# Last layer norm of a hybrid encoder step: the products by the scale moved from VectorE to GpSimd for all row blocks but the last, whose Newton steps go to GpSimd

## The chip, the core and the metric

The kernel runs on one core of a Trainium2 chip. The metric is device time in microseconds (us); lower is better. Engines are named as in the profile: PE is TensorE (matmuls), PEld its weight loads, DVE is VectorE, ACT is ScalarE, POOL is GpSimd, SP is SyncE, whose queue issues the transfers between the core's memory (SBUF) and DRAM.

## The reference, cut to what matters

One layer of an encoder trunk for two groups of requests: 1024 prompt tokens and 8 x 16 sample tokens, 1152 rows of 1024 features in all. Three mixers (windowed attention and two linear recurrences) read one projection and are merged; a layer norm; a feed-forward part with 2816 hidden features; a second layer norm, whose result is the output. All inputs and outputs are float32.

```python
def layer_norm(x, g, b):
    xf = x.astype(F32)
    mu = xf.mean(-1, keepdims=True)
    var = jnp.square(xf - mu).mean(-1, keepdims=True)
    return ((xf - mu) * lax.rsqrt(var + LN_EPS) * g.astype(F32) + b.astype(F32)).astype(x.dtype)
...
    up, new_ffn_conv = causal_dwconv(x @ w_up, buf_ffn, f_conv_w)
    gate, val = jnp.split(up + f_conv_b, 2, axis=-1)
    x = layer_norm(ALPHA * x + (jax.nn.silu(gate) * val) @ w_down, ln2_g, ln2_b)
```

Only this last `layer_norm` is touched by the change.

## The kernel before

The 1152 tokens are nine row blocks of 128 (`NT` = 9): blocks 0 to 7 are the prompt, block 8 is the sample. In the feed-forward part the hidden features stand on partitions; the down-projection then brings the tokens back onto partitions. Its sums are kept in SBUF, in nine tiles `yac` of 128 tokens x 1024 features.

The hidden features are taken 256 at a time; the last call of `down` takes the last 512 of them. For each row block and each half of 512 columns it runs twelve matmuls into a PSUM bank (tag `g`, five banks in this phase), and VectorE adds the bank to `yac` (L1758). Behind each row block stands `beside(last_ln(j))`: the layer norm of that block is a generator that is moved on in steps between the matmuls of the blocks that follow. `yield 3` in it lets three such steps pass.

In `last_ln` of blocks 0 to 7:

- `normalise` takes the statistics of both halves on VectorE (L321), joins them (L322), adds the epsilon (L324), and computes the inverse root in `rsqrt`: an integer seed (L302, L303) and three Newton steps of three VectorE operations each (L307, L308, L310), all on 128x1; then `shifted` makes -mean/deviation (L331), and ScalarE scales and shifts the block (L336).
- Three VectorE products by the scale `g2` (L1787) and three POOL additions of `b2` (L1788) follow, on thirds of 384, 384 and 256 columns, then one store of 512 KB.

Block 8 has nothing behind it and has its own branch: the statistics and Newton steps on VectorE at raised priority, `(y - mean) g` in three VectorE operations (L1779), `times 1/deviation, plus b` in three more (L1781), and a store after each third.

The order on each engine is laid down when the kernel is built: a scheduler with its own timeline places the instructions of all engines, and each engine then takes its queue strictly in that order, waiting on semaphores. In the kernel before, the scheduler interleaves the Newton steps of one block with the additions and statistics of the next ones.

Of the kernel before, what the change touches and what calls it, by code (L numbers as in the profile page):

```python
# [10 lines left out]
F32 = mybir.dt.float32  # L11
F32R = mybir.dt.float32r
I32 = mybir.dt.int32
# [4 lines left out]
P = 128  # L18
# [27 lines left out]
def shape_constants():  # L46
    c = np.zeros((P, CW), np.float32)
    s = np.arange(P)[:, None]
    t = np.arange(P)[None, :]

    def put(n, v):
        o, w = CO[n]
        c[:, o:o + w] = v

    put("ident", s == t)
    put("ui", s <= t)
    same = (s // TB) == (t // TB)
    put("us", (s <= t) & same)
    put("bm", same)
    put("negp", np.where(s <= t, 0.0, -1e30))  # L60
    put("negs", np.where((s <= t) & same, 0.0, -1e30))
    k = np.arange(2 * P)[None, :]
    put("nega", np.where(((s < 64) & (k >= 192)) | ((s >= 64) & (k < 64)), -1e30, 0.0))
    # s in the first half of a pair of blocks of b, t in its second half; columns for the second halves alone
    for b in (1, 2, 4, 8, 16):
        r = ((s // (2 * b)) == (t // (2 * b))) & ((s // b) % 2 == 0)
        put(f"r{b}", r.reshape(P, -1, 2, b)[:, :, 1].reshape(P, 64))
    return c
# [3 lines left out]
def tile_encoder_step(ctx: ExitStack, tc: tile.TileContext, cst, x_prompt, x_sample, cache_k, cache_v, st_hgrn,  # L72
# [18 lines left out]
    # the banks of PSUM, shared out anew for each phase  # L91
# [22 lines left out]
    def load_in_turn(out, in_):  # L114
        """not ahead of the loads that come before"""
        tc.keep_in_program_order(nc.sync.dma_start(out=out, in_=in_))

# [35 lines left out]
    def halves_of(x, b):  # L153
        """[P, a, 128] -> [P, a, pairs, 2, b]"""
        return x.rearrange("p a (n h t) -> p a n h t", h=2, t=b)

    def put_seconds(x, b, ps):
        """the columns of the second halves, where s lies in the first half of the same pair"""
        m = x.shape[1]
        V.copy_predicated(halves_of(x, b)[:, :, :, 1, :],  # L160
                          reg(b).rearrange("p (o n t) -> p o n t", o=1, t=b).to_broadcast([P, m, 64 // b, b]),
                          ps.rearrange("p a (n t) -> p a n t", t=b))
# [6 lines left out]
    # per-feature vectors, features on partitions  # L169
# [29 lines left out]
    def prep(pieces, kt=KD, cols=P):  # L199
        """pieces: (part of the raw tile, DRAM view [p, k, c]); the exact two-part split of the weights"""  # L200
        raw = wp.tile([P, KD, P], F32, tag="wraw", name=nm("wraw"), bufs=2)
        for sel, ap in pieces:
            load(sel(raw), ap)
        hl = wp.tile([P, 2, KD, P], F32R, tag="whl", name=nm("whl"), bufs=2)
        S.copy(hl[:, 0, :kt, :cols], raw[:, :kt, :cols])  # L205
        V.tensor_sub(hl[:, 1, :kt, :cols], raw[:, :kt, :cols], hl[:, 0, :kt, :cols].bitcast(F32))  # L206
        return hl
# [5 lines left out]
    # work that runs beside the large products: generators, moved on between their parts  # L213
# [18 lines left out]
    def block(hl, xh, xl, n, evict, kt=KD):  # L232
        """features on partitions: [128 columns of the weights, 384 tokens]"""
# [11 lines left out]
    def row_block(lh, ll, rhs, evict):  # L245
        """tokens on partitions: [128 tokens, 512 columns of the weights]"""
# [10 lines left out]
    class Queue:  # L257
        """Blocks of the large products in order; the weights of the next unit are made ahead."""
# [40 lines left out]
    def rsqrt(pool, x, n):  # L299
        """x ** -0.5 on [P, n]: an integer seed and three Newton steps"""  # L300
# [13 lines left out]
    def ln_group(pool, tiles, eps):  # L314
        """tiles: for each, its two halves of 512 features, tokens on partitions -> means and 1 / deviation"""
# [12 lines left out]
    def shifted(pool, mu, rs):  # L328
        """-mean / deviation"""
# [8 lines left out]
    def to_features(pool, xns, n, gname, bname, hi, lo):  # L338
        """normalised rows of three tiles -> scaled, features on partitions, in two parts"""
# [12 lines left out]
    # -mean / deviation and 1 / deviation of each input row: the residual is made anew from the input  # L352
# [40 lines left out]
    def bc(x, n, w=P):  # L393
        """[P, n] -> [P, n, w]"""
        return x.rearrange("p (c o) -> p c o", o=1).to_broadcast([P, n, w])

    def rowb(x, n, w=P):
        """[P, w] -> [P, n, w]"""
# [5 lines left out]
    # ======== A: banded attention with sinks ========  # L404
# [28 lines left out]
    # the first two units: the tokens that are ready first  # L433
# [23 lines left out]
    # the norm weights carry the half of silu = x (1 + tanh(x/2)) / 2  # L457
# [27 lines left out]
    def a_parts(j):  # L485
        """queries: their two parts on the two halves of the partitions; keys: the first part on both halves, and
        the second; so a product of 128 rows and one of 64 make a score"""
# [160 lines left out]
    # ======== common to B and C ========  # L648
    # group n: tokens 384 n..; its units of 128 tokens; in the last group the third unit is the samples
# [3 lines left out]
    def ev_silu2(store_to, tag, bufs):  # L653
        """x (1 + tanh(x/2)): twice silu"""
# [7 lines left out]
    def finish_group(oT, fac, wcol, z2, out):  # L662
        """o in rows per token -> normalised, gated, features on partitions"""
# [14 lines left out]
    def sample_cross(st, pair):  # L678
        """[P, b, n, 16] against each sample's state -> features on partitions, PSUM [v, b, n, 16]"""
# [6 lines left out]
    def sample_state(st, el, kT, w, out):  # L686
        """S_b <- e_b S_b + k_b^T w_b, and out it goes"""
# [11 lines left out]
    # ======== C: gated delta rule ========  # L699
    cg = {}  # L700

    def c_gates():
# [45 lines left out]
        # softplus: max(x, 0) + log1p(exp(-|x|))  # L748
# [42 lines left out]
    def ev_conv(ci, pre_fn, done):  # L791
        """causal convolution of width 4 and twice silu; the pieces follow one another"""
# [64 lines left out]
    def c_units(hd):  # L857
        """v, q, k; the gate z comes later"""
# [13 lines left out]
    def c_pre(hd, n):  # L872
# [9 lines left out]
        # norms of q and k (twice silu both)  # L882
# [18 lines left out]
        # the rows (v - e^cum k S) / |k| go through (I + N)^-1 with N = (k k^T dec) beta / |k|^2 by columns,  # L901
        # then times beta / |k|: w of the reference
# [13 lines left out]
        # v in rows per token (twice silu), by |k|  # L916
# [5 lines left out]
        # decays between tokens, [s, t]  # L922
# [22 lines left out]
        # (I - M)^-1: blocks of 16 by substitution, a block per partition  # L945
# [38 lines left out]
    def c_levels(hd, n):  # L984
# [15 lines left out]
        # 16 -> 32  # L1000
# [18 lines left out]
        # 32 -> 64  # L1019
# [16 lines left out]
        # 64 -> 128  # L1036
# [89 lines left out]
    def c_finish(hd, n):  # L1126
        x, h = hd.g[n], hd.h
        # q was left unnormalised: n = o rq' rsqrt(rq'^2 mean(o^2) + eps), rq' = rq / sqrt(128)
# [10 lines left out]
    # ======== B: gated linear attention with a decay per key feature ========  # L1139
    def b_consts():  # L1140
# [6 lines left out]
        # lower bounds: softmax over the layers, running sum less the first layer's  # L1147
# [13 lines left out]
    def b_units(hd):  # L1161
# [3 lines left out]
        # f = lb + (1 - lb) sigmoid(x) = (1 + lb e) / (1 + e) with e = exp(-x), at least 1e-30  # L1165
# [34 lines left out]
    def b_pre(hd, n):  # L1200
# [10 lines left out]
        # q and k against the ends of the chunk  # L1211
# [20 lines left out]
        # s = t, and neighbours  # L1232
# [25 lines left out]
    def b_levels(hd, n):  # L1258
        """every pair (s, t) of a chunk at the level whose halves part it"""
# [88 lines left out]
    def b_finish(hd, n):  # L1348
        x, h = hd.g[n], hd.h
        # o is doubled  # L1350
# [5 lines left out]
    # ======== the order of the mixers ========  # L1356
# [114 lines left out]
    def branch_units(br, follow):  # L1471
        """the parts of the next branch's o take the place of this one's"""
# [36 lines left out]
    def pair(m, dst):  # L1509
        """w_branch rows of the last branch, columns of blocks m and m + 1"""  # L1510
# [40 lines left out]
    def rows_h(j):  # L1551
        """the residual, doubled as the mix is"""
# [11 lines left out]
    def mix_split(stage):  # L1564
        """mix = mh + ml; a step uses two pieces and frees one, each n of the branch before has freed eight"""
# [206 lines left out]
    def last_ln(j):  # L1772
        y = yac[j]
        if j == NT - 1:
            # nothing follows: each third goes out as it is ready, ((y - mean) g) / deviation + b
            with tc.high_priority(400):
                (mu, rs), = ln_group(fp, [[y[:, :512], y[:, 512:]]], LN_EPS)
                for sl, gg in zip(thirds, g2):
                    V.scalar_tensor_tensor(y[:, sl], y[:, sl], mu, gg, ALU.subtract, ALU.mult)  # L1779
                for sl, bb in zip(thirds, b2):  # L1780
                    V.scalar_tensor_tensor(y[:, sl], y[:, sl], rs, bb, ALU.mult, ALU.add)  # L1781
                    store(y_s.rearrange("b t d -> (b t) d")[:, sl], y[:, sl])
            return
        normalise(fp, y, LN_EPS)
        yield 3
        for sl, gg, bb in zip(thirds, g2, b2):
            V.tensor_mul(y[:, sl], y[:, sl], gg)  # L1787
            G.tensor_add(y[:, sl], y[:, sl], bb)  # L1788
        store(y_p[0, j * P:(j + 1) * P, :], y)

    pairs = [ffn_pair(i) for i in range(NFF)]
    # the first two units: the tokens that are ready first
# [47 lines left out]
```

## Time and profile before

| | |
|---|---|
| time, median of 3 runs | 2320.24 us (2312.8 to 2323.56) |
| span of the profiled execution | 2315.3 us |
| busy share of PE / DVE / ACT / POOL over the span | 97% / 65% / 40% / 4% |
| granted TensorE clock, mean | 0.988 |
| last normalise step of block 7 on ACT starts | 2304.97 us |

For the profiled execution only the span, from its first to its last instruction, is recorded; no time of its own stands beside it. Times in the traces are us from the start of the span. A row of single instructions has start, duration, engine, line, operation, `written<-read` and the tile's shape; in brackets stands how long the engine had been idle before it and what ended that. On VectorE successive rows overlap a little, so the distance from start to start says what an instruction costs the queue.

### The profile page before, as it was taken

The page shows a single profiled execution, that of the slowest core. Times are in us where ns is not written, and L with a number is a line of the kernel's source. Part 1 is how long each engine was busy: PE and PEld are TensorE (multiplying, and loading weights), DVE is VectorE, ACT ScalarE, POOL GpSimd, SP SyncE. Part 2 cuts the span into 40 slices and gives each one's busy share as a digit, 9 for nine tenths or more (in the row PEclk, how much of TensorE's full clock was granted, in tenths as well). Part 3 has the DMA queues.
Part 4 walks back from the last instruction along what each step waited for, and adds up shares of the span by engine and source line. Part 5 has one row for each costly group of instructions (what it writes and reads, how often), then busy time and mean ns, then how long its engine had stood idle before and what let it go on. Part 6 is the DMA issues. An engine that isn't in the chain of part 4 may idle for free.

```text
span 2315.3 us, 35344 instructions
## 1 busy us (share of the span) xinstructions
PE 2256.6 (97%) x13297; PEld 2101.9 (91%) x13297; DVE 1504.4 (65%) x4324; ACT 927.5 (40%) x2106; POOL 102.8 (4%) x74
## 2 busy tenths in 40 slices
PE   6999999999999999999999999999999999999996
PEld 6988989999999999999999978999999999999994
DVE  7256446667675657766777797676566566656669
ACT  4356434434344446354532333453334333432331
POOL 2000000000000000000000054000000000000004
PEclk9999989999999999999999999999999999999998
DMA  4111222222222221222354552321111110111112
GB/s 132 46 55 43 80 74 62 65 80 67 63 82 60 70 63 54 68 66 78 98 151 134 174 165 74 139 65 47 38 29 56 47 47 21 56 52 42 38 47 82
DMA packets 223836, 168.46 MB, mean 73 GB/s; under 512 B 34427, under 2 KB 213409, under 8 KB 223649
## 3 DMA queue, kind: packets, MB, share of 16 engines
q1 hardware_dynamic: 223664, 166.21, 24.0%
q8 instruction: 104, 1.70, 0.3%
q14 instruction: 68, 0.55, 0.1%
HBM read 126.91 MB, written 40.11 MB: 72 GB/s over the span
## 4 chain that ended last, share of the span: by engine, by line
PE 87%; DVE 7%; ACT 3%; DMA 2%; issue 1%; SPq 0%; POOL 0%; DVEq 0%; ACTq 0%
PE psg L107 72%; PE psp L107 6%; PE psch L107 4%; PE psp L147 2%; PE psms L107 2%; PE psch L147 1%; PE psms L147 1%; DVE yac L1787 1%; DVE lnst L321 1%; DMA x<-d_g 1%; ACT L1185 1%; ACT L1181 0%; DVE nwa L308 0%; DVE nwy L310 0%; DVE whl L206 0%
## 5 line engine op out<-in xcount | busy, mean ns | idle before, releaser
L107 PE MATMUL psg<-hh,whl 128*128 128x384 f32 x2976 | 812.6, 346 | 0.0
L107 PE MATMUL psg<-x1h,whl 128*128 128x384 f32 x2112 | 545.0, 336 | 1.2 <-ACT whl L205 1.2
L107 PEld LDWEIGHTS psg<-hh,whl 128*128 128x128 f32 x2976 | 537.7, 189 | 8.7 <-issue 3.6
L107 PE MATMUL psg<-hl,whl 128*128 128x384 f32 x1488 | 511.3, 344 | 1.5 <-POOL hl L347 1.3
L107 PEld LDWEIGHTS psg<-x1h,whl 128*128 128x128 f32 x2112 | 382.8, 188 | 3.2 <-ACT whl L205 1.5
L107 PE MATMUL psg<-x1l,whl 128*128 128x384 f32 x1056 | 355.5, 337 | 0.6 <-POOL x1l L347 0.6
L107 PEld LDWEIGHTS psg<-hl,whl 128*128 128x128 f32 x1488 | 281.5, 189 | 5.1 <-POOL hl L347 1.6
L107 PE MATMUL psg<-late,g 128*128 128x512 f32 x1080 | 251.2, 391 | 0.0
L107 PEld LDWEIGHTS psg<-late,g 128*128 128x128 f32 x1080 | 201.9, 188 | 42.9
L107 PEld LDWEIGHTS psg<-x1l,whl 128*128 128x128 f32 x1056 | 198.9, 188 | 1.7 <-POOL x1l L347 0.9
L206 DVE TENSOR_TENSOR whl<-wraw,whl 128x1024 fp32r<-128x1024 f32 (+1 forms) x122 | 144.2, 1183 | 68.0 <-ACT whl L205 66.9
L1758 DVE TENSOR_TENSOR yac<-yac,psg 128x512 f32<-128x512 f32 x180 | 123.5, 687 | 91.4 <-PE psg L107 88.0
L107 PE MATMUL psg<-o,whl 128*128 128x384 f32 x720 | 140.1, 345 | 3.1 <-DVE x L1464 1.7
L205 ACT CAST whl<-wraw 128x1024 fp32r<-128x1024 f32 (+1 forms) x122 | 121.4, 995 | 48.0 <-PE psg L107 24.7
L107 PEld LDWEIGHTS psg<-o,whl 128*128 128x128 f32 x720 | 125.8, 191 | 6.7 <-issue 2.1
L107 PE MATMUL psg<-wres,mixh 128*128 128x512 f32 x288 | 92.8, 395 | 3.6 <-DVE x L1464 2.7
L1718 DVE SCALAR_TENSOR_TENSOR va<-xp,fvec,va 128x384 f32<-128x384 f32 x132 | 82.0, 622 | 19.8 <-ACT va L1715 18.1
L1718 DVE SCALAR_TENSOR_TENSOR ga<-xp,fvec,ga 128x384 f32<-128x384 f32 x132 | 81.6, 620 | 8.2 <-ACT ga L1715 6.6
L1747 ACT CAST late<-wraw 128x1024 fp32r<-128x1024 f32 x20 | 20.1, 1047 | 162.6 <-PE psg L107 162.6
L1699 ACT COPY xp<-psg 128x384 f32<-128x384 f32 x88 | 42.2, 480 | 107.0 <-PE psg L107 106.8
L1399 ACT ACTIVATE ga<-psg 128x384 f32<-128x384 f32 x72 | 35.3, 491 | 104.0 <-PE psg L107 88.6
L1556 POOL TENSOR_TENSOR rows<-rows,gbin 128x1024 f32<-128x1024 f32 x9 | 27.7, 3078 | 1087.0 <-ACT rows L1555 1087.0
(449 smaller groups left out, 3260.1 us busy)
## 6 DMA issues: line engine op xcount, KB each, us to landing
wraw<-in_w_in_dram SPq DMA_DIRECT2D x58, 512.0 KB
wraw<-in_w_up_dram SPq DMA_DIRECT2D x44, 512.0 KB
d_g<-ga SPq DMA_DIRECT2D x72, 192.0 KB
wraw<-in_w_down_dram SPq DMA_DIRECT2D x22, 512.0 KB
acc<-d_g SPq DMA_DIRECT2D x48, 192.0 KB
d_o<-sq SPq DMA_DIRECT2D x24, 192.0 KB
xp<-d_o SPq DMA_DIRECT2D x24, 192.0 KB
x<-d_g SPq DMA_DIRECT2D x24, 192.0 KB
```

Of the source, the lines that this page charges most:

```text
L107: PE.matmul(out, lhsT, rhs, start=start, stop=stop)
L147: PE.transpose(out, in_, ident[:n, :n])
L205: S.copy(hl[:, 0, :kt, :cols], raw[:, :kt, :cols])
L206: V.tensor_sub(hl[:, 1, :kt, :cols], raw[:, :kt, :cols], hl[:, 0, :kt, :cols].bitcast(F32))
L321: V.bn_stats(out=st[:, i, :], in_=s_)
L1185: S.activation(s_, hd.f[n], AF.Exp, scale=-1.0)
L1399: S.activation(g, ps, AF.Tanh, scale=0.5)
L1556: G.tensor_mul(t, t, gb[:, 0])
L1699: S.copy(xp[:, 2:2 + NW], ps)
L1718: V.scalar_tensor_tensor(acc[:, :w], xp[:, j:j + w], fvec[:, j, ct:ct + 1], acc[:, :w], ALU.mult, ALU.add)
L1758: lambda ps: V.tensor_add(yac[j][:, cs], yac[j][:, cs], ps))
L1787: V.tensor_mul(y[:, sl], y[:, sl], gg)
```

## The change

Three things, all in `last_ln`:

- Blocks 0 to 7: after `normalise`, the three products by `g2` are issued on POOL, each followed by POOL's addition of `b2`. The generator pauses two steps instead of three.
- Block 8: the statistics stay on VectorE, written out in place. The Newton steps go to a new function `newton`: seed on VectorE (three operations), three steps of four POOL operations each. The scheduler can place VectorE's three products by `g2` beside them.
- The second half of block 8, `times 1/deviation, plus b`, and its stores are as before.

Elsewhere only comments and docstrings are gone.

```diff
     def last_ln(j):
+
         y = yac[j]
-        if j == NT - 1:
-            # nothing follows: each third goes out as it is ready, ((y - mean) g) / deviation + b
-            with tc.high_priority(400):
-                (mu, rs), = ln_group(fp, [[y[:, :512], y[:, 512:]]], LN_EPS)
-                for sl, gg in zip(thirds, g2):
-                    V.scalar_tensor_tensor(y[:, sl], y[:, sl], mu, gg, ALU.subtract, ALU.mult)
-                for sl, bb in zip(thirds, b2):
-                    V.scalar_tensor_tensor(y[:, sl], y[:, sl], rs, bb, ALU.mult, ALU.add)
-                    store(y_s.rearrange("b t d -> (b t) d")[:, sl], y[:, sl])
+        if j < NT - 1:
+            normalise(fp, y, LN_EPS)
+            yield 2
+            for sl, gg, bb in zip(thirds, g2, b2):
+                G.tensor_mul(y[:, sl], y[:, sl], gg)
+                G.tensor_add(y[:, sl], y[:, sl], bb)
+            store(y_p[0, j * P:(j + 1) * P, :], y)
             return
-        normalise(fp, y, LN_EPS)
-        yield 3
-        for sl, gg, bb in zip(thirds, g2, b2):
-            V.tensor_mul(y[:, sl], y[:, sl], gg)
-            G.tensor_add(y[:, sl], y[:, sl], bb)
-        store(y_p[0, j * P:(j + 1) * P, :], y)
+
+        with tc.high_priority(400):
+            mv = fp.tile([P, 2], F32, tag="lnmv", name=nm("lnmv"), bufs=3)
+            st = fp.tile([P, 2, 6], F32, tag="lnst", name=nm("lnst"), bufs=3)
+            for i in range(2):
+                V.bn_stats(out=st[:, i, :], in_=y[:, 512 * i:512 * (i + 1)])
+            V.bn_aggr(out=mv, in_=st)
+            mu, rs = mv[:, 0:1], newton(mv[:, 1:2])
+            for sl, gg in zip(thirds, g2):
+                V.scalar_tensor_tensor(y[:, sl], y[:, sl], mu, gg, ALU.subtract, ALU.mult)
+            for sl, bb in zip(thirds, b2):
+                V.scalar_tensor_tensor(y[:, sl], y[:, sl], rs, bb, ALU.mult, ALU.add)
+                store(y_s.rearrange("b t d -> (b t) d")[:, sl], y[:, sl])
+
+    def newton(var):
+
+        x, i, a, y = (fp.tile([P, 1], t, name=nm("nt")) for t in (F32, I32, F32, F32))
+        V.tensor_scalar_add(x, var, LN_EPS)
+        V.tensor_scalar(i, x.bitcast(I32), 1, None, ALU.logical_shift_right)
+        V.tensor_scalar(i, i, -1.0, 1597463007.0, ALU.mult, ALU.add)
+        v = i.bitcast(F32)
+        for _ in range(3):
+            G.tensor_mul(a, v, v)
+            G.tensor_mul(a, a, x)
+            G.tensor_scalar(a, a, -0.5, 1.5, ALU.mult, ALU.add)
+            G.tensor_mul(y, a, v)
+            v = y
+        return y
```

In the changed kernel the products of blocks 0 to 7 are L1779, the additions L1780, block 8's halves L1792 and L1794, its seed L1800 to L1802 and its Newton steps L1805 to L1808. What the scheduler makes of it is best seen in the queues. The numbers behind a name tell its buffers apart: `yac_16747`, `yac_16785`, `yac_16826` and `yac_16862` are blocks 4 to 7, `ln2v_23433` to `23437` the scale, `ln2v_23439` to `23443` the shift.

VectorE's queue before, from the seed of block 6 (`lnvr_23808`) on:

```order
L302 TENSOR_SCALAR nwi_23810<-lnvr_23808 128x1
L307 TENSOR_TENSOR nwa_23760<-nwy_23758 128x1
L303 TENSOR_SCALAR nwi_23810<-nwi_23810 128x1
L308 SCALAR_TENSOR_TENSOR nwa_23760<-nwa_23760,lnvr_23745 128x1
L307 TENSOR_TENSOR nwa_23813<-nwi_23810 128x1
L310 SCALAR_TENSOR_TENSOR nwy_23763<-nwa_23760,nwy_23758 128x1
L308 SCALAR_TENSOR_TENSOR nwa_23813<-nwa_23813,lnvr_23808 128x1
L331 SCALAR_TENSOR_TENSOR lnnb_23765<-lnmv_23740,nwy_23763 128x1
L310 SCALAR_TENSOR_TENSOR nwy_23816<-nwa_23813,nwi_23810 128x1
L1758 TENSOR_TENSOR yac_16826<-yac_16826,psg_23838 128x512
```

The same part of VectorE's queue now, from block 5's L331 on; after the last row shown come L307, L308, the second addition of block 7, L310, the statistic and block 6's L331:

```order
L331 SCALAR_TENSOR_TENSOR lnnb_23765<-lnmv_23740,nwy_23763 128x1
L322 BN_AGGR lnmv_23803<-lnst_23804 128x2
L324 TENSOR_SCALAR lnvr_23808<-lnmv_23803 128x1
L302 TENSOR_SCALAR nwi_23810<-lnvr_23808 128x1
L303 TENSOR_SCALAR nwi_23810<-nwi_23810 128x1
L307 TENSOR_TENSOR nwa_23813<-nwi_23810 128x1
L1758 TENSOR_TENSOR yac_16826<-yac_16826,psg_23796 128x512
L308 SCALAR_TENSOR_TENSOR nwa_23813<-nwa_23813,lnvr_23808 128x1
L321 BN_STATS lnst_23867<-yac_16826 128x6
L310 SCALAR_TENSOR_TENSOR nwy_23816<-nwa_23813,nwi_23810 128x1
L307 TENSOR_TENSOR nwa_23818<-nwy_23816 128x1
L308 SCALAR_TENSOR_TENSOR nwa_23818<-nwa_23818,lnvr_23808 128x1
```

The two blocks' Newton chains no longer alternate: one block's chain stands alone, and each step reads what the step before it wrote. POOL's queue now, one period (products of block 5, the last addition of block 4, additions of block 5), where before it had three additions:

```order
L1779 TENSOR_TENSOR yac_16785<-yac_16785,ln2v_23433 128x384
L1779 TENSOR_TENSOR yac_16785<-yac_16785,ln2v_23435 128x384
L1779 TENSOR_TENSOR yac_16785<-yac_16785,ln2v_23437 128x256
L1780 TENSOR_TENSOR yac_16747<-yac_16747,ln2v_23443 128x256
L1780 TENSOR_TENSOR yac_16785<-yac_16785,ln2v_23439 128x384
L1780 TENSOR_TENSOR yac_16785<-yac_16785,ln2v_23441 128x384
```

An addition never stands right behind the product that it needs, and the last addition of a block stands behind the products of the next. The end of POOL's queue, with block 8's first Newton operations (`nt`):

```order
L1779 TENSOR_TENSOR yac_16862<-yac_16862,ln2v_23437 128x256
L1780 TENSOR_TENSOR yac_16826<-yac_16826,ln2v_23443 128x256
L1805 TENSOR_TENSOR nt_23992<-nt_23991 128x1
L1780 TENSOR_TENSOR yac_16862<-yac_16862,ln2v_23439 128x384
L1780 TENSOR_TENSOR yac_16862<-yac_16862,ln2v_23441 128x384
L1780 TENSOR_TENSOR yac_16862<-yac_16862,ln2v_23443 128x256
L1806 TENSOR_TENSOR nt_23992<-nt_23992,nt_23990 128x1
L1807 TENSOR_SCALAR nt_23992<-nt_23992 128x1
L1808 TENSOR_TENSOR nt_23993<-nt_23992,nt_23991 128x1
```

The additions of block 7 stand between the first Newton operation and the other eleven; the first one waits for VectorE's seed, which stands in VectorE's queue behind its three L1792. On SP the store of block 7 now stands ahead of block 8's three, where it stood behind them; every other transfer is where it was.

## The prediction

> **What bounds the kernel now.** I read the table of busy time by stage first, then the chain of waits, then the single instructions of the last 60 us. Columns of the table: stretch, its length, busy us (instructions) of PE, PEld, DVE, ACT, POOL, granted clock, DMA share, GB/s.
>
> ```profile
> 2271.50:2278.00 6.50, 6.50 (x30) 5.29 (x29) 6.50 (x23) 1.24 (x1) 3.07 (x3) 1.00 0.20 81
> 2291.00:2297.40 6.40, 1.28 (x6) 0.71 (x4) 6.40 (x23) 1.24 (x1) 3.06 (x3) 0.86 0.23 92
> 2297.40:2304.00 6.60, 0.00 (x0) 0.00 (x0) 6.60 (x18) 1.24 (x1) 2.99 (x3) 0.50 0.22 88
> 2304.00:2315.30 11.30, 0.00 (x0) 0.00 (x0) 6.75 (x22) 1.24 (x1) 3.44 (x3) 0.50 0.34 130
> ```
>
> TensorE sets the pace of the program almost to the end, but its last product is over at 2291.00 + 1.28 = 2292.3, and 23 us follow. From about 2260 VectorE is the bound: it is busy in every us, and POOL less than half the time. What a row block costs VectorE, and how busy that time really is, stands in the single rows (start, duration, engine, line):
>
> ```profile
> 2260.51 0.55 DVE L1787 TENSOR_TENSOR yac<-yac,ln2v 128x384 f32<-128x384 f32 x1
> ...
> 2286.38 0.55 DVE L1787 TENSOR_TENSOR yac<-yac,ln2v 128x384 f32<-128x384 f32 x1
> 2286.85 0.55 DVE L1787 TENSOR_TENSOR yac<-yac,ln2v 128x384 f32<-128x384 f32 x1
> 2287.01 1.27 POOL L1788 TENSOR_TENSOR yac<-yac,ln2v 128x384 f32<-128x384 f32 x1 [3.40 <-DVE yac L1787]
> 2287.32 1.25 DVE L1787 TENSOR_TENSOR yac<-yac,ln2v 128x256 f32<-128x256 f32 x1
> 2288.24 1.21 POOL L1788 TENSOR_TENSOR yac<-yac,ln2v 128x384 f32<-128x384 f32 x1
> 2288.61 0.86 DVE L310 SCALAR_TENSOR_TENSOR nwy<-nwa,nwy 128x1 f32<-128x1 f32 x1
> 2289.39 0.68 DVE L1758 TENSOR_TENSOR yac<-yac,psg 128x512 f32<-128x512 f32 x1
> 2289.41 0.74 POOL L1788 TENSOR_TENSOR yac<-yac,ln2v 128x256 f32<-128x256 f32 x1
> 2289.99 0.14 DVE L324 TENSOR_SCALAR lnvr<-lnmv 128x1 f32<-128x1 f32 x1
> ...
> 2299.21 0.55 DVE L1787 TENSOR_TENSOR yac<-yac,ln2v 128x384 f32<-128x384 f32 x1
> ```
>
> Six blocks take 2299.21 - 2260.51 = 38.70, so 6.45 us each. The third product, the smallest, takes 1.25 where its larger fellows take 0.55, and a Newton step on 128x1 takes 0.86: each ends as a POOL addition ends (2288.24, 2289.41). The addition L1758, one operand from PSUM, starts in time and takes 0.68 beside POOL.
>
> **What the change meets.** The change makes POOL run back to back, which this kernel does once already, at the first layer norm:
>
> ```profile
> 1404.46 1.02 POOL L347 TENSOR_TENSOR x1l<-x,x1h 128x384 fp32r<-128x384 f32 x1 [3.05 <-DVE x1h L346]
> 1405.44 2.42 POOL L1556 TENSOR_TENSOR rows<-rows,gbin 128x1024 f32<-128x1024 f32 x1
> 1405.89 0.69 DVE L321 BATCH_NORM_STATS2 lnst<-rows 128x6 f32<-128x512 f32 x1
> 1406.62 0.21 DVE L322 BATCH_NORM_AGGREGATE lnmv<-lnst 128x2 f32<-128x12 f32 x1
> 1406.86 0.15 DVE L324 TENSOR_SCALAR lnvr<-lnmv 128x1 f32<-128x1 f32 x1
> 1407.05 0.15 DVE L302 TENSOR_SCALAR nwi<-lnvr 128x1 int32<-128x1 int32 x1
> 1407.24 0.15 DVE L303 TENSOR_SCALAR nwi<-nwi 128x1 int32<-128x1 int32 x1
> 1407.43 0.45 DVE L307 TENSOR_TENSOR nwa<-nwi 128x1 f32<-128x1 f32 x1
> 1407.91 0.16 DVE L308 SCALAR_TENSOR_TENSOR nwa<-nwa,lnvr 128x1 f32<-128x1 f32 x1
> 1407.94 2.42 POOL L1557 TENSOR_TENSOR rows<-rows,gbin 128x1024 f32<-128x1024 f32 x1
> 1408.10 2.27 DVE L310 SCALAR_TENSOR_TENSOR nwy<-nwa,nwi 128x1 f32<-128x1 f32 x1
> 1410.31 2.41 POOL L1556 TENSOR_TENSOR rows<-rows,gbin 128x1024 f32<-128x1024 f32 x1
> 1410.40 2.33 DVE L307 TENSOR_TENSOR nwa<-nwy 128x1 f32<-128x1 f32 x1
> 1412.77 0.16 DVE L308 SCALAR_TENSOR_TENSOR nwa<-nwa,lnvr 128x1 f32<-128x1 f32 x1
> 1412.80 2.41 POOL L1557 TENSOR_TENSOR rows<-rows,gbin 128x1024 f32<-128x1024 f32 x1
> ```
>
> Statistics, aggregate and the operations with one tensor operand (L324, L302, L303) run at 0.15 to 0.69 while POOL is busy. Each operation on two SBUF tensors (L307, L308, L310, and L331 by its form) that arrives during a POOL operation ends with it, though it has one element per partition. Where POOL's next operation needs the result before it (L1557 after L1556), two such steps get in between; where it doesn't (L1556 at 1410.31 after L1557), one does, and the next, 0.03 later, waits again. By the Trainium skill, SBUF — State Buffer, section on who interferes with whom, a VectorE instruction with two SBUF inputs and a GpSimd instruction that reads SBUF exclude each other for the whole instruction, and the loser blocks. The trace agrees (2.27 and 2.33 us for one element), and this rule speaks against the change.
>
> **The change, part by part.** *Removed from VectorE:* three products per block, by their rows from 2286.38 to 2287.32 + 1.25 = 2288.57, so 2.2 us of the 6.45. *Added to POOL:* three products beside its three additions. By start-to-start distances a 384 wide one takes 1405.44 - 1404.46 = 0.98; the 256 wide one, by the same 0.04 off its duration, 0.74 - 0.04 = 0.70. Products and additions alike, since L1556 and L1557 last 2.42 both. A block's six make 4 x 0.98 + 2 x 0.70 = **5.32 us**, less than 6.45: POOL could keep up. By the Trainium skill, Perfetto Trace Analysis, section on the GPSIMD instruction, a GpSimd duration in the profile isn't to be trusted and the start-to-start distance is. With durations (1.02, 0.74) the six would make 5.56, the sum below 1.4 us more.
>
> *Where the stall goes.* VectorE keeps ten two-tensor operations per block (nine Newton, one L331), in a chain in which each needs the one before, and POOL now has six operations queued with no dependence on their direct predecessor. So I take one VectorE step per POOL operation. The walk of a period, in the order of the changed program, from L331 of block j:
> - L331 starts ACT 0.19 later (rows below), ACT takes 1.24, POOL reacts in about 0.08 (2287.01 against the product's end at 2286.93): POOL's burst begins at **1.51**. Until then VectorE does aggregate, L324, two seed steps, L307 (0.93 by the 0.24 and 0.19 distances above) and the addition L1758 (to 1.60).
> - Burst, **5.32**. L308, L310, L307, L308, L310 and L307 are let through one per POOL operation; only one statistic fits between them.
> - After it: L308 0.04, addition 0.07, L310 0.60, statistic 0.12, next L331 0.60: **1.44**.
>
> Period 1.51 + 5.32 + 1.44 = 8.27 against 6.45. VectorE loses its 2.2 us of products and gains 8.27 - (6.45 - 2.2) = 4.0 us of waiting.
>
> *Its start.* Blocks 0 and 1 differ. POOL has five operations in block 0's burst (4.62, the sixth is queued behind block 1's products): L331 comes 1.51 + 4.62 + 0.23 = 6.36 later. Next interval: no seed steps, so one Newton step gets in before the burst, which ends the wait with it: 1.51 + 5.32 + 0.66 = 7.49.
>
> ```profile
> 2258.63 0.16 DVE L331 SCALAR_TENSOR_TENSOR lnnb<-lnmv,nwy 128x1 f32<-128x1 f32 x1
> 2258.83 1.25 ACT L336 ACTIVATE yac<-yac,lnnb,nwy 128x1024 f32<-128x1024 f32 x1 [11.25 <-DVE lnnb L331]
> ...
> 2304.78 0.15 DVE L331 SCALAR_TENSOR_TENSOR lnnb<-lnmv,nwy 128x1 f32<-128x1 f32 x1
> 2304.97 1.24 ACT L336 ACTIVATE yac<-yac,lnnb,nwy 128x1024 f32<-128x1024 f32 x1 [5.92 <-DVE lnnb L331]
> ```
>
> Up to 2258.63 nothing moves. L331 of block 7, before at 2304.78, comes at 2258.63 + 6.36 + 7.49 + 5 x 8.27 = 2313.8: **+9.0 us**.
>
> *The tail.* Before, 2315.3 - 2304.78 = 10.5 us follow this L331. Now (from it): aggregate and L1800 to 0.44; three products L1792 0.44 to 1.70 (0.47, 0.47, 0.32), in which POOL's first product of block 7 waits; seeds to 2.05, hidden. POOL from 1.70: three products 2.66, block 6's last addition 0.70, one Newton step, then **three additions of block 7, 2.66, which stand in POOL's queue ahead of the other eleven Newton steps**. A 128x1 step on POOL isn't in the trace. From 1024 and 384 wide (2.42, 1.02) the straight line leaves 0.18 at zero width, and dependent operations follow with a gap of 0.08 (1405.44 + 2.42 = 1407.86 to 1407.94): 0.25 each, my value, since the form is the same. The lower bound is 0.16, VectorE's L308; the upper one 0.74, a whole 256 wide addition: -1.1 to +5.9 us over twelve. At 0.25 the twelve are 3.0; they end at 1.70 + 2.66 + 0.70 + 2.66 + 3.0 = 10.7. The three L1794, POOL now still, 0.05 + 0.47 + 0.47 + 0.47: 12.2. From the last VectorE result to the end:
>
> ```profile
> 2310.66 0.47 DVE L1781 SCALAR_TENSOR_TENSOR yac<-yac,nwy,ln2v 128x256 f32<-128x256 f32 x1
> 2311.68 0.39 SPq L110 DMA_DIRECT2D out_dram<-yac  x1
> 2313.50:2314.00 0.50, 0.00 (x0) 0.00 (x0) 0.00 (x0) 0.00 (x0) 0.00 (x0) 0.50 0.71 279
> ```
>
> Before it is 2315.3 - 2311.1 = 4.2 us, as the 512 KB of block 7 are stored last (issued 2311.68). That store now goes first, behind POOL's additions and ahead of the sample's thirds on SP; the last is a third, 128 KB for 512 KB, some 1.3 us shorter by the 1.9 us in which the large one lands (2312.0 to 2313.9). Tail 12.2 + 2.9 = 15.1 for 10.5: **+4.6**. The 2.7 of it for block 7's additions and the Newton steps behind them were covered by VectorE's own steps before.
>
> Sum: 9.0 + 4.6 = **+13.6 us** on 2315.3, span 2328.9. The span lies 5 us below the median of the runs, 2320.24, within their spread (2312.8 to 2323.56); on the median the forecast is **2333.8**, taken as 2333.
>
> **Rivals.** *(a) Two VectorE steps per POOL operation*, as where POOL's operations depend on each other. For it: the pairs at 1407.43/1407.91. Against: 1410.40, and the alternation at 2287 to 2289. Then the period is the burst plus its start, 6.87 (7.0 less over five), and the first two intervals 1.9 shorter each: +13.6 - 10.8 = +2.8, time 2323. *(b) Not slower: small steps don't wait and TensorE is the bound.* VectorE's period unblocked is 4.7, POOL's 5.3; TensorE's is four groups of six matmuls, 2287.96 - 2286.58 = 1.38 apart, so 5.5:
>
> ```profile
> 2286.58 1.54 PE L107 MATMUL psg<-late,g 128*128 128x512 f32 x6
> 2287.96 1.55 PE L107 MATMUL psg<-whl,g 128*128 128x512 f32 x6
> ```
>
> The last addition would come at 2292.3, L331 at 2293.7, plus 15.1: span 2308.8, time about 2313. It decides if POOL lets a step in at once; the waits of 0.86 and 2.3 us speak against it. *(c) Slower yet*: Newton steps at 0.37 (+1.4) and POOL delayed 0.1 by each step let through (+0.6 per period, +4): 2339.
>
> **How the numbers follow.** Forecast 0.62 (2327 to 2340, from period and step errors of 0.4 and the runs' spread), (a) 0.18, (b) 0.08, (c) 0.12. The range 2319 to 2342 leaves out (b) and edges. A measurement here tells 0.5%, 11.6 us, from nothing. The forecast lies just beyond: some 0.4 of its 0.62 is slower, with (c) 0.52; (a) and the rest of it, and most of (b), are no change, 0.46; faster 0.02.
>
> **What would show it.** L331 from block 2 to 7 at 8.3 us (rivals 6.9, 5.5), ten two-tensor steps per block of which six last 0.6 to 1.0; POOL still for 2 to 3 us per block; twelve Newton steps on POOL 0.25 apart, the second only after block 7's additions; TensorE now waiting for VectorE's additions. Wrong, if Newton steps on VectorE stay at 0.16 beside a busy POOL, or if POOL's queue never empties.

## The result

| | before | changed |
|---|---|---|
| time, median of 10 runs each | 2319.44 us | 2330.02 us (2323.07 to 2336.48) |
| ratio | 1 | 1.0052, 95% interval 1.0038 to 1.0066 |
| span of the profiled execution | 2315.3 us | 2321.3 us |
| from block 0's L331 to the end of the span | 56.7 us | 69.2 us |

The change makes the kernel slower by 0.5%, 10.6 us by the medians. The ratios here and below are of fast runs alone; one slow run was left out, 3959.84 us in experiment 5. The two profiled executions differ by only 6.0 us, because the changed one reached the last layer norm 6.5 us earlier (its first L331 starts at 2252.10, before at 2258.63) and is the fastest of its ten runs. So I compare stretches that begin at block 0's L331, the first point that the change can move (up to it the instructions of TensorE, ScalarE and GpSimd are the same in both, and VectorE's but for two neighbours that changed places): 69.2 against 56.7, **+12.5 us** where the prediction had +13.6.

Single rows of the changed kernel's timeline, L331 of blocks 0 to 4 and of block 7 (start, duration, engine, line):

```profile
2252.10 0.16 DVE L331 SCALAR_TENSOR_TENSOR lnnb<-lnmv,nwy 128x1 f32<-128x1 f32 x1
...
2258.36 0.16 DVE L331 SCALAR_TENSOR_TENSOR lnnb<-lnmv,nwy 128x1 f32<-128x1 f32 x1
...
2264.87 0.45 DVE L331 SCALAR_TENSOR_TENSOR lnnb<-lnmv,nwy 128x1 f32<-128x1 f32 x1
...
2273.32 0.14 DVE L331 SCALAR_TENSOR_TENSOR lnnb<-lnmv,nwy 128x1 f32<-128x1 f32 x1
...
2281.61 0.14 DVE L331 SCALAR_TENSOR_TENSOR lnnb<-lnmv,nwy 128x1 f32<-128x1 f32 x1
...
2306.16 0.14 DVE L331 SCALAR_TENSOR_TENSOR lnnb<-lnmv,nwy 128x1 f32<-128x1 f32 x1
```

The distances are 6.26, 6.51, 8.45 and 8.29, and the last three average 8.18 ((2306.16 - 2281.61) / 3). One whole period, from just behind block 4's L331 on (rows that repeat a burst are left out):

```profile
2283.11 1.02 POOL L1779 TENSOR_TENSOR yac<-yac,ln2v 128x384 f32<-128x384 f32 x1 [2.95 <-ACT yac L336]
...
2283.20 0.93 DVE L308 SCALAR_TENSOR_TENSOR nwa<-nwa,lnvr 128x1 f32<-128x1 f32 x1
...
2284.66 0.45 DVE L310 SCALAR_TENSOR_TENSOR nwy<-nwa,nwi 128x1 f32<-128x1 f32 x1
2285.05 0.74 POOL L1779 TENSOR_TENSOR yac<-yac,ln2v 128x256 f32<-128x256 f32 x1
2285.14 0.67 DVE L307 TENSOR_TENSOR nwa<-nwy 128x1 f32<-128x1 f32 x1
...
2287.41 0.99 POOL L1780 TENSOR_TENSOR yac<-yac,ln2v 128x384 f32<-128x384 f32 x1
2287.50 0.91 DVE L307 TENSOR_TENSOR nwa<-nwy 128x1 f32<-128x1 f32 x1
2288.45 0.16 DVE L308 SCALAR_TENSOR_TENSOR nwa<-nwa,lnvr 128x1 f32<-128x1 f32 x1
2288.53 0.68 DVE L1758 TENSOR_TENSOR yac<-yac,psg 128x512 f32<-128x512 f32 x1
...
2289.85 0.14 DVE L331 SCALAR_TENSOR_TENSOR lnnb<-lnmv,nwy 128x1 f32<-128x1 f32 x1
```

Six Newton steps on one element per partition last 0.45 to 0.93 while POOL's burst runs (2283.11 to 2288.40). Each ends about when a POOL operation ends, and the next waits that one out as well: it is issued within 0.1 us of the next POOL operation's start, but for the one at 2284.66, which stands behind a statistic. Before and behind the burst the same operations take 0.16, and the addition L1758 never waits. POOL then stands still for 2.95 us, since ACT's input to it waits for the next L331. The statement of the Trainium skill that the prediction weighed (SBUF — State Buffer, section on who interferes with whom) holds here for operands of one element: 0.93 us beside a POOL operation of 1.02.

The table of busy time by stage (stretch, length, then busy us and instructions of PE, PEld, DVE, ACT, POOL, granted clock, DMA share, GB/s):

```profile
2264.00:2280.00 16.00, 16.00 (x71) 12.86 (x69) 15.41 (x34) 2.49 (x2) 11.81 (x14) 1.00 0.19 78
2296.00:2304.00 8.00, 0.00 (x0) 0.00 (x0) 7.69 (x19) 1.24 (x1) 5.05 (x7) 0.50 0.15 59
```

VectorE reads busy for 7.69 of 8 us with 19 instructions. Before it had 18 in 6.6 us, among them the three wide products by `g2` that have gone to POOL. The busy share has not told waiting from work.

The tail of the changed kernel, from block 8's first Newton step on POOL; the row at 2313.15 is block 7's last addition:

```profile
2311.11 0.19 POOL L1805 TENSOR_TENSOR nt<-nt 128x1 f32<-128x1 f32 x1
...
2313.15 0.72 POOL L1780 TENSOR_TENSOR yac<-yac,ln2v 128x256 f32<-128x256 f32 x1
2313.83 0.19 POOL L1806 TENSOR_TENSOR nt<-nt,nt 128x1 f32<-128x1 f32 x1
2314.11 0.19 POOL L1807 TENSOR_SCALAR nt<-nt 128x1 f32<-128x1 f32 x1
...
2316.57 0.19 POOL L1808 TENSOR_TENSOR nt<-nt,nt 128x1 f32<-128x1 f32 x1
2316.80 0.62 DVE L1794 SCALAR_TENSOR_TENSOR yac<-yac,nt,ln2v 128x384 f32<-128x384 f32 x1 [7.61 <-POOL nt L1808]
```

The second Newton step comes 2.72 us after the first, behind three additions. The eleven that are left are 0.27 apart, and VectorE stands idle for 7.61 us until the last of them.

### The profile page after: what moved, and what is told of

Same layout as the page of the kernel before. It is cut to its first block, busy times and chain, and to the rows that moved or that the text cites. A ratio compares the mean times of both kernels' runs of the same rounds, so it can differ in the third digit from the quotient of the medians.

```text
span 2321.3 us, 35353 instructions
## 1 busy us (share of the span) xinstructions
PE 2251.4 (97%) x13297; PEld 2096.5 (90%) x13297; DVE 1509.7 (65%) x4291; ACT 927.8 (40%) x2106; POOL 122.4 (5%) x110
## 4 chain that ended last, share of the span: by engine, by line
PE 87%; DVE 6%; ACT 3%; DMA 2%; issue 1%; POOL 0%; SPq 0%; DVEq 0%; POOLq 0%; ACTq 0%
PE psg L107 72%; PE psp L107 6%; PE psch L107 4%; PE psp L147 2%; PE psms L107 2%; PE psch L147 1%; PE psms L147 1%; DVE nwa L308 1%; DVE nwa L307 1%; DVE nwy L310 1%; DMA x<-d_g 1%; DVE lnst L321 1%; DMA wraw<-in_w_out_dram 0%; ACT L1185 0%; DVE whl L206 0%
## 5 line engine op out<-in xcount | busy, mean ns | idle before, releaser
L1758 DVE TENSOR_TENSOR yac<-yac,psg 128x512 f32<-128x512 f32 x180 | 123.6, 687 | 91.4 <-PE psg L107 87.9
```

Source lines behind the costliest of these rows:

```text
L1758: lambda ps: V.tensor_add(yac[j][:, cs], yac[j][:, cs], ps))
```

## The experiments

In all of them "m/d" is the last small operation of a block on VectorE (-mean/deviation; L331 before and in the change, L340 or L339 where lines were added). The columns: ratio to the kernel before with its interval; us from block 0's m/d to the end of the span; mean distance of m/d from block 2's to block 6's; us from block 7's m/d to the end. Where the ratio is missing there is one run alone, and it tells nothing of the time; its trace is read for the distances.

| kernel | ratio | first m/d to end | per block | last m/d to end |
|---|---|---|---|---|
| before | 1 | 56.7 | 6.42 | 10.5 |
| changed | 1.0052 [1.0038, 1.0066] | 69.2 | 8.28 | 15.1 |
| 1 products only | 1.0058 [1.0040, 1.0077] | 69.6 | 8.28 | 15.5 |
| 2 Newton steps only | 1.0006 [0.9994, 1.0018] | 56.9 | 6.42 | 10.7 |
| 3 changed, one-tensor steps | 1.0003 [0.9989, 1.0017] | 53.9 | 5.47 | 14.0 |
| 4 changed, halves on POOL | one run | 66.8 | 7.28 | 18.9 |
| 5 before, one-tensor steps | **0.9959** [0.9945, 0.9973] | 49.9 | 6.02 | 10.5 |
| 6 products only, one-tensor steps | 0.9994 [0.9980, 1.0008] | 51.3 | 5.47 | 11.5 |
| 7 as 6, block 7 on VectorE | 0.9984 [0.9969, 0.9999] | 51.1 | 5.47 | 11.2 |
| 8 as 6, blocks 6 and 7 on VectorE | 0.9976 [0.9966, 0.9987] | 50.5 | 5.47 | 10.5 |
| 9 as 6, m/d on two tensors | one run | 52.6 | 5.89 | 11.4 |
| 10 as 6, addition behind its product | 0.9996 [0.9978, 1.0014] | 51.4 | 5.47 | 15.1 |

### 1 and 2: each part alone

In the first, blocks 0 to 7 are as changed and block 8 as before; in the second, the reverse:

```diff
 # 1: block 8 of the changed kernel
-            mu, rs = mv[:, 0:1], newton(mv[:, 1:2])
+            (mu, rs), = ln_group(fp, [[y[:, :512], y[:, 512:]]], LN_EPS)
 # 2: blocks 0 to 7 of the changed kernel
-                G.tensor_mul(y[:, sl], y[:, sl], gg)
+                V.tensor_mul(y[:, sl], y[:, sl], gg)
```

> The products of blocks 0 to 7 on POOL as in the change; block 8 keeps all its Newton steps on VectorE, as before the change. Theory (a VectorE operation on two SBUF tensors waits for the POOL operation that is running, and one gets in per POOL operation): L331 of blocks 2 to 7 again 8.2 us apart, and block 8's nine Newton steps on VectorE now wait too, behind the seven POOL operations of block 7 that are queued then; tail from block 7's L331 to the end about 15 us, so the whole about 12 us slower than before, as the change. Rival (the change's 4.6 us in the tail come from the Newton steps on POOL): tail 10.5 us, the whole 8 us slower.

> Block 8's Newton steps on POOL as in the change; the products of blocks 0 to 7 stay on VectorE, as before the change. Theory: L331 of blocks 2 to 7 stays 6.45 us apart; twelve POOL steps of 0.27 us, of which the last stands behind block 7's additions; tail about 10 us against 10.5: no difference to before, within 1 us. Rival (Newton steps on POOL are a loss of their own of some 4 us): 3 to 5 us slower than before.

The products alone bring the whole loss (69.6 us, period 8.28). The Newton steps alone bring nothing that can be measured. The first one's tail, with block 8's Newton steps on VectorE again:

```profile
2323.98 0.92 DVE L307 TENSOR_TENSOR nwa<-nwy 128x1 f32<-128x1 f32 x1
...
2325.88 0.65 DVE L310 SCALAR_TENSOR_TENSOR nwy<-nwa,nwy 128x1 f32<-128x1 f32 x1
2326.56 0.16 DVE L307 TENSOR_TENSOR nwa<-nwy 128x1 f32<-128x1 f32 x1
```

They wait for POOL's burst as those of the other blocks do, and free steps of 0.16 come only when it is over. So the tail is 15.5 us with block 8's steps on VectorE and 15.1 with them on POOL. The prediction's tail term belongs to block 7's six POOL operations, whichever engine runs the Newton steps behind or beside them: with the products on VectorE and the Newton steps on POOL (experiment 2) the tail is 10.7 us.

### 3: is it the second tensor?

The changed kernel, with every small VectorE step of blocks 0 to 7 in this layer norm written as an operation that reads one tensor and takes the other value as a per-partition scalar (`fp` is the pool of tiles of this layer norm; block 8's Newton steps stay on POOL as they are):

```diff
+            if n == 1 and pool.name == "fp":
...
+                V.tensor_scalar(a, y, y, None, ALU.mult)
+                V.tensor_scalar(a, a, x, -0.5, ALU.mult, ALU.mult)
...
+                V.tensor_scalar(y2, a, 1.5, y, ALU.add, ALU.mult)
...
-        V.scalar_tensor_tensor(nb, mu, -1.0, rs, ALU.mult, ALU.mult)
+        if pool.name == "fp":
+            V.tensor_scalar(nb, mu, -1.0, rs, ALU.mult, ALU.mult)
```

> The change, with the Newton steps of blocks 0 to 7 written as operations on one tensor and a scalar per partition (tensor_scalar with a [128, 1] operand) in place of two tensors: the same values, as many instructions, the chain as before. Theory (it is the second SBUF tensor that waits for POOL): no step over 0.3 us beside a busy POOL, L331's successor (L340) 5.5 us apart, TensorE's pace; block 8 with its POOL steps behind block 7 unchanged, tail 15 us: 6 us faster than before, so 18 us faster than the change. Rival (the loss of the interleaved order of the Newton chains makes VectorE slow, or the scalar operand waits as well): 8.2 us apart, 12 us slower than before.

The mechanism is confirmed, the time is missed. With POOL at work, single rows of this kernel (a row that ends in x2 puts two operations together):

```profile
2289.24 1.98 POOL L1790 TENSOR_TENSOR yac<-yac,ln2v 128x384 f32<-128x384 f32 x2
2289.28 0.21 DVE L308 TENSOR_SCALAR nwa<-nwy 128x1 f32<-128x1 f32 x1
2289.53 0.21 DVE L309 TENSOR_SCALAR nwa<-nwa,lnvr 128x1 f32<-128x1 f32 x1
2289.78 0.21 DVE L311 TENSOR_SCALAR nwy<-nwa,nwy 128x1 f32<-128x1 f32 x1
...
2291.84 1.01 POOL L1791 TENSOR_TENSOR yac<-yac,ln2v 128x384 f32<-128x384 f32 x1
...
2291.93 5.54 DVE L1803 SCALAR_TENSOR_TENSOR yac<-yac,lnmv,ln2v 128x384 f32<-128x384 f32 x1
...
2296.32 0.74 POOL L1791 TENSOR_TENSOR yac<-yac,ln2v 128x256 f32<-128x256 f32 x1
...
2298.38 0.20 DVE L340 TENSOR_SCALAR lnnb<-lnmv,nwy 128x1 f32<-128x1 f32 x1
```

Three steps run within one POOL operation, 0.21 each, and blocks come 5.53 apart, which is TensorE's pace. One block's Newton chain stands alone here as in the change, so it isn't the lost interleaving that made the change slow. But the first operation on two tensors that now meets POOL, block 8's product L1803, waits **5.54 us**, through six POOL operations until POOL's queue is empty, and holds up block 7's m/d in VectorE's queue. That, and the 14.0 us tail with the Newton steps behind block 7's additions, are why only 2.8 us are gained on the kernel before by the stretches (56.7 to 53.9), where 6 were expected, and nothing that the ratio can tell; on the change it is 15.3 us. The Trainium skill says of a bf16 scale or an int32 index given as such a per-partition scalar that it "does not take up the second tensor stream" (DVE: scalar operands, raw-bit mode, write accounting and state across instructions, section on scalar operands); 0.21 us beside a busy POOL shows the same here for float32 scalars.

### 4: how many steps are let in

The changed kernel with each POOL operation cut into two halves; the sums are the same, the count doubles:

```diff
-                G.tensor_mul(y[:, sl], y[:, sl], gg)
-                G.tensor_add(y[:, sl], y[:, sl], bb)
+                h = (sl.stop - sl.start) // 2
+                for c in (slice(0, h), slice(h, 2 * h)):
+                    G.tensor_mul(y[:, sl][:, c], y[:, sl][:, c], gg[:, c])
+                for c in (slice(0, h), slice(h, 2 * h)):
+                    G.tensor_add(y[:, sl][:, c], y[:, sl][:, c], bb[:, c])
```

> The change with every POOL product and addition of blocks 0 to 7 cut in two (192, 192, 192, 192, 128, 128 columns): twelve operations per block in place of six, so more POOL work by the fixed share of each. Theory (one VectorE step per POOL operation, however short): a waiting step ends after 0.4 to 0.55 us in place of 0.66 to 0.94, POOL's burst grows from 5.3 to some 6.2 us, and L331 of blocks 2 to 7 still comes sooner than in the change, 7.7 us apart for 8.2. Rival (VectorE loses in proportion to the time that POOL is busy): later than in the change, 8.5 us and more apart.

```profile
2289.13 0.59 POOL L1783 TENSOR_TENSOR yac<-yac,ln2v 128x192 f32<-128x192 f32 x1
2289.22 0.52 DVE L308 SCALAR_TENSOR_TENSOR nwa<-nwa,lnvr 128x1 f32<-128x1 f32 x1
2289.77 0.53 DVE L310 SCALAR_TENSOR_TENSOR nwy<-nwa,nwy 128x1 f32<-128x1 f32 x1
2290.24 0.60 POOL L1783 TENSOR_TENSOR yac<-yac,ln2v 128x192 f32<-128x192 f32 x1
2290.34 0.52 DVE L307 TENSOR_TENSOR nwa<-nwy 128x1 f32<-128x1 f32 x1
```

The waits shrink with the POOL operation (0.59 for 1.02), from 0.92 to 0.52, and the period from 8.28 to 7.28 (7.7 was expected), although twelve halves take POOL longer than six wholes (8 x 0.55 + 4 x 0.42 = 6.1 us by start-to-start distances for 5.3). So one step is let in per POOL operation, whatever its length; a share of POOL's time it is not. The tail grew to 18.9 us, as the Newton steps on POOL now stand behind more operations of blocks 6 and 7.

### 5: the steps alone, products left on VectorE

The kernel before with experiment 3's edit of the small steps, and nothing else.

> The kernel before with the one-tensor Newton steps alone, products on VectorE. Theory: the one step per block that waits 0.8 us for POOL's second addition no longer does, the third product still waits; 5.7 us per block for 6.45, so 4 to 5 us faster than before. Rival (the step's wait was in VectorE's slack or moves to another instruction): no difference.

This has the shortest time of all kernels: 2308.99 us (the median of all seven runs), 0.9959 of before, some 9.5 us by that ratio. Its rows beside a POOL addition:

```profile
2277.66 0.69 DVE L1769 TENSOR_TENSOR yac<-yac,psg 128x512 f32<-128x512 f32 x1 [0.44 <-PE psg L107]
...
2279.85 1.60 POOL L1791 TENSOR_TENSOR yac<-yac,ln2v 128x384 f32<-128x384 f32 x1 [2.32 <-DVE yac L1790]
2280.16 0.42 DVE L1790 TENSOR_TENSOR yac<-yac,ln2v 128x256 f32<-128x256 f32 x1
...
2280.55 0.21 DVE L308 TENSOR_SCALAR nwa<-nwy 128x1 f32<-128x1 f32 x1
```

More than expected was gained. In blocks 1 to 5 the smallest product no longer waits either: 0.42 where it took 1.22 to 1.25 before, with the POOL addition (1.55 to 1.60) now the one that is held up. I had counted the steps alone. In blocks 0, 6 and 7 it still takes 1.21 to 1.24. Why the two engines changed places in five blocks isn't shown: the product comes 0.25 to 0.31 us behind the start of the addition in these, and 0.24 to 0.37 in the other three and in the kernel before. The stretch from block 0's m/d on is 6.8 us shorter, within the ratio's interval (6.3 to 12.8 us). VectorE now waits for TensorE (0.44): in the middle of this layer norm the bound is TensorE's pace, m/d of blocks 1 to 5 coming 5.04, 5.69, 5.45 and 5.61 apart, and from block 7 on the tail of 10.5 us is as before. The 6.02 in the table includes 7.32 before block 6's m/d, which here stands behind block 8's three products; block 7's then follows 3.84 later.

### 6 to 8: can moved products still pay?

Experiment 6 is 3 with block 8 as before; 7 and 8 also keep block 7, or blocks 6 and 7, whole on VectorE (7 is shown):

```diff
+            E = G if j < 7 else V
-                G.tensor_mul(y[:, sl], y[:, sl], gg)
-                G.tensor_add(y[:, sl], y[:, sl], bb)
+                E.tensor_mul(y[:, sl], y[:, sl], gg)
+                E.tensor_add(y[:, sl], y[:, sl], bb)
```

> As the run with one-tensor steps, and block 8's branch as before the change, so its Newton steps are one-tensor steps on VectorE too. Theory: L340 5.5 us apart; POOL is last, with block 7's additions over some 11 us after TensorE's end, then its store: 8 us faster than before (a candidate for the best version). Rival (as in the run before it): 12 us slower.

> One-tensor steps everywhere, products on POOL for blocks 0 to 6, block 7's products and additions both on VectorE. Theory: VectorE keeps TensorE's pace of 5.5 us per block, but block 8's first two-tensor product stands behind POOL's additions of blocks 5 and 6 and waits some 5 us, as it did in the two runs with POOL's queue full; block 7 no longer waits for POOL: 7 us faster than before. Rival (that wait was block 7's doing): 11 us faster.

> As the run before it, with block 6's products and additions on VectorE too, so that POOL is done when block 8's two-tensor operations come. Theory: no wait for POOL at the end, VectorE's 2.5 us for block 6 are added: 11 us faster than before, 0.5% (a candidate for the best version). Rival (the added VectorE work costs what the wait did): 7 us faster, as the run before it.

All three run at TensorE's pace up to block 6, and in all three the first product that VectorE then makes on two tensors meets a POOL at work and waits until its queue is empty: 5.54 us in 6, 5.57 in 7, and in 8:

```profile
2291.92 3.51 DVE L1791 TENSOR_TENSOR yac<-yac,ln2v 128x384 f32<-128x384 f32 x1
...
2292.38 1.01 POOL L1792 TENSOR_TENSOR yac<-yac,ln2v 128x384 f32<-128x384 f32 x1
...
2294.29 0.72 POOL L1792 TENSOR_TENSOR yac<-yac,ln2v 128x256 f32<-128x256 f32 x1
```

So each gave less than expected (8, 7 and 11 us), and none is faster than experiment 5. That 8 is slower than 5 isn't shown: the intervals of their ratios overlap, and the stretches differ by 0.6 us.

### 9 and 10: what makes a wait of 5.5 us

Experiment 9 is 6 with one small step, m/d, on two tensors again (L339). Experiment 10 is 6 with each POOL addition directly behind the product that it needs, so that POOL pauses between them.

```diff
 # 10
-                G.tensor_mul(y[:, sl], y[:, sl], gg)
-                G.tensor_add(y[:, sl], y[:, sl], bb)
+                tc.keep_in_program_order(G.tensor_mul(y[:, sl], y[:, sl], gg))
+                tc.keep_in_program_order(G.tensor_add(y[:, sl], y[:, sl], bb))
```

> The products-on-GpSimd kernel with one-tensor Newton steps on VectorE (block 8 as before), but the last of a block's ten small operations, -mean/deviation on 128x1, is again one that reads two SBUF tensors. Question: what made block 8's first product wait 5.54 us for six GpSimd operations, its width (384 per partition) or that GpSimd was running back to back for a long time with nobody let in. If width: the small operation waits for one GpSimd operation at most, under 1 us, its starts stay 5.5 to 5.7 us apart from block to block (TensorE's pace), and the span is within 1 us of 2310.5. If the long run: it waits until GpSimd's queue is empty, several us in at least some blocks; a period is then GpSimd's own six operations and its start, 5.32 + 1.51 = 6.8 us, five such periods cost 5 x 1.3 = 6.5 us, and the span is about 2317.

> The products-on-GpSimd kernel with one-tensor Newton steps on VectorE (block 8 as before), with each GpSimd addition directly behind the product that it needs, so that GpSimd pauses by about 0.08 us between a product and its addition. If block 8's first product on VectorE waits for a pause in GpSimd's queue: it is let in at the first pause, within 1 us, in place of 5.54 us, and -mean/deviation of block 7 comes about 4.5 us sooner; span about 2306, time about 2311 (0.996 to 0.997 of before). GpSimd's six operations last 5.3 + 3 x 0.08 = 5.6 us, level with TensorE's 5.5. If it is the order in which the two engines ask, and pauses do not matter: again about 5.5 us of waiting, span 2310.5, time 2315.5 (0.999 of before).

In 9, m/d of blocks 4 to 6:

```profile
2271.62 3.52 DVE L339 SCALAR_TENSOR_TENSOR lnnb<-lnmv,nwy 128x1 f32<-128x1 f32 x1
...
2274.37 0.75 POOL L1787 TENSOR_TENSOR yac<-yac,ln2v 128x256 f32<-128x256 f32 x1
...
2279.73 0.44 DVE L339 SCALAR_TENSOR_TENSOR lnnb<-lnmv,nwy 128x1 f32<-128x1 f32 x1
...
2284.60 0.87 DVE L339 SCALAR_TENSOR_TENSOR lnnb<-lnmv,nwy 128x1 f32<-128x1 f32 x1
```

Width is out: one element waited 3.52 us, until POOL's queue was empty (2274.37 + 0.75 = 2275.12), and in experiment 6 block 8's second operations of the same width (L1800, from 2301.64 on) got in after one POOL operation each, in 1.29, 1.07 and 1.21 us. Two other m/d here got in after one POOL operation too. The long undisturbed run isn't the answer either. POOL had run without a pause for 5.1 us since it let block 3's m/d in (2266.32, 0.19 us) when block 4's was kept out, but also for 5.1 us since block 2's (2261.04, 0.18 us) when block 3's got in at once. And block 8's product came at 2290.02, only 4.6 us after a step had been let in, and waited 5.25 us. Neither time was met: the stretch is 1.3 us longer than in 6.

In 10, block 8's product:

```profile
2291.11 0.99 POOL L1791 TENSOR_TENSOR yac<-yac,ln2v 128x384 f32<-128x384 f32 x1
...
2291.50 1.02 DVE L1798 SCALAR_TENSOR_TENSOR yac<-yac,lnmv,ln2v 128x384 f32<-128x384 f32 x1
2292.06 1.04 POOL L1790 TENSOR_TENSOR yac<-yac,ln2v 128x256 f32<-128x256 f32 x1
...
2305.17 0.72 POOL L1791 TENSOR_TENSOR yac<-yac,ln2v 128x256 f32<-128x256 f32 x1
```

1.02 us in place of 5.54, and m/d of block 7 came 3.6 us sooner (8.35 us after block 6's, 11.95 in experiment 6; 4.5 were expected). But it wasn't a pause that let the product in. It got in when the addition L1791 ended (2291.11 + 0.99 = 2292.10), and POOL's next operation, the product L1790 at 2292.06, doesn't need that addition and followed without a gap. The pause between the last product and its addition was over (2291.04 to 2291.11) before VectorE's product was issued. So the run doesn't say why the wait was short here.

The time wasn't as expected either. POOL is now what is waited for: it runs from 2259.71 to 2305.89 without standing still, 46.2 us, where in experiment 6 it took 45.8 with 2.88 idle. The 24 pauses that it was given make 1.9 us together, and VectorE holds some of its operations up (1.04 us for 0.72 at 2292.06). So the additions end no sooner, and the tail is 15.1 for 11.5.

## Why the prediction was right, and where it was off

It named slower as likelier and 2333 us; it came out slower, at 2330.02, within the forecast's own 2327 to 2340, and by the mechanism that it had named. Step by step:

- **One step per POOL operation.** Right, and shown by experiments 3 (no second tensor: 0.21 us), 4 (half the operation: half the wait) and 1 (the products alone). Rivals (a), two steps per operation, and (b), steps that don't wait, needed 6.87 and 5.5 per block; the period is 8.2. The 4.7 us that (b) gives VectorE itself is added up nowhere; in experiment 6, with one-tensor steps, it is some 4.9 (5.53 less 0.66 of idle). One reading was loose: the third product (1.25 us) doesn't end with POOL's addition but 0.3 us behind it (2288.57 against 2287.01 + 1.27 = 2288.28), so it was let in there and then did its work.
- **The period.** Predicted 8.27, measured 8.29 to 8.15 for the last four. Its parts from block 4's L331 at 2281.61: burst after 1.50 (predicted 1.51), 5.29 long to 2288.40 (5.32), and 1.45 behind it (1.44; its five terms add up to 1.43).
- **The start.** First interval 6.26 for 6.36. The second was **mis-sized**: 6.51 for 7.49. I took one Newton step to run before that burst; three did, so L331 itself was the sixth operation to be let in:

```profile
2259.03 0.15 DVE L308 SCALAR_TENSOR_TENSOR nwa<-nwa,lnvr 128x1 f32<-128x1 f32 x1
...
2259.76 0.14 DVE L310 SCALAR_TENSOR_TENSOR nwy<-nwa,nwi 128x1 f32<-128x1 f32 x1
...
2259.94 0.16 DVE L307 TENSOR_TENSOR nwa<-nwy 128x1 f32<-128x1 f32 x1
```

  This is nearly all of the gap between +7.9 us (2306.16 - 2252.10 less the 46.15 of before) and the predicted +9.0.
- **The tail.** 15.1 as predicted, for 10.5. The Newton steps were put at 0.25 and are 0.27 apart; they end 10.6 us after L331 (10.7), and the end of L1794 is followed by 3.0 us (2.9). The first product on POOL was to wait for VectorE's third; it was the other way round (1.28 us), which cost nothing.
- **TensorE would wait for VectorE's additions.** Hardly: it waited once, for 0.80 us.

```profile
2281.01 1.65 PE L107 MATMUL psg<-late,g 128*128 128x512 f32 x6 [0.80 <-DVE yac L1758]
```

  Its last product is over at 2286.84, 34.7 us after block 0's L331, before 33.7. I didn't count the banks. Five additions were still to come behind it (2288.53, 2290.85, 2296.68, 2299.01, 2304.84), as many as `g` has banks in this phase, so nearly all of VectorE's lag fits into them. The sum isn't touched, since the path ran through VectorE anyway.
- **The offset to the median.** I took the profiled execution of before as 5 us under the median and added that to the forecast. Some 1.8 us of these only say that a time is longer than its span (2323.07 and 2321.3 for the changed kernel's). Against the medians the offset was fair: 1.0052 x 2320.24 is 2332.3, and the stretch is 1.1 us shorter than forecast.

What remains open is the rule by which POOL lets VectorE in. It was right for the steps of this change, one per operation. The waits of 3.5 to 5.6 us in experiments 3 and 6 to 9 don't follow it, and none of the experiments says what decides between the two.

## What to carry to other kernels

Before work is moved to GpSimd to relieve VectorE, look at what VectorE keeps: if that reads two SBUF tensors, even for one element per partition, it was paced by GpSimd's operations here (0.45 to 0.93 us for 0.16), and the relief turned into a larger wait. Small per-partition arithmetic is better written with a one-tensor operation and a per-partition scalar; here that alone was worth 0.4%, and no move of the products added to it. A VectorE that reads 96% busy (7.69 of 8 us) should be counted in instructions and their unhindered durations before it is taken for a full one.

## What the runs showed of the hardware that I had not expected

- An operation on two SBUF tensors can be kept out for much longer than one GpSimd operation: 5.54 us (experiments 3 and 6), 5.57 (7), 5.25 and 3.52 (9), 3.51 (8), each until GpSimd's queue was empty. In 6 and 9 others got in after one GpSimd operation. Neither the width of the operation (3.52 us for one element; 1.07 to 1.29 for 384 or 256 in experiment 6) nor the length of GpSimd's undisturbed run before it (in at once after 5.1 us, kept out after 4.6, both in 9) decides it. What does is open.
- The reverse happens too. In the kernel before, a GpSimd operation that takes 2.42 us alone came among VectorE's operations on two tensors that followed each other closely:

```profile
1353.17 6.52 POOL L1556 TENSOR_TENSOR rows<-rows,gbin 128x1024 f32<-128x1024 f32 x1 [4.06 <-ACT rows L1555]
```

- A Newton step of one element per partition costs GpSimd 0.19 us, and a chain of them 0.27 us each, close to VectorE's own one-tensor steps (0.21, 0.25 apart in experiment 3).
